# Encoder trunk: the gate and up weight sums, their loads' queue, and how the fourth sum is formed

## The chip, the cores and the metric

The kernel runs on one core of one Trainium2 chip. The metric is device time of one launch in microseconds. The profiler's page and views come from one execution of it.

## The reference, cut to what matters

A two-layer encoder on 528 tokens (16 learned meta tokens and 512 inputs) of width 1024. Each layer is a feed-forward block, a mixer (gated linear attention beside softmax attention), and a second feed-forward block:

```python
def swiglu(x, w_gate, w_up, w_down):
    return (jax.nn.silu(x @ w_gate) * (x @ w_up)) @ w_down

for l in range(DEPTH):
    h = h + 0.5 * swiglu(rmsnorm(h, norm_gains[l, 0]),
                         ffn_w_gate[l, 0], ffn_w_up[l, 0], ffn_w_down[l, 0])
    h = h + mixer(rmsnorm(h, norm_gains[l, 1]), w_in[l], ...)
    h = h + 0.5 * swiglu(rmsnorm(h, norm_gains[l, 2]),
                         ffn_w_gate[l, 1], ffn_w_up[l, 1], ffn_w_down[l, 1])
return rmsnorm(h, final_norm)[:, N_META:]
```

So there are four feed-forward blocks, with D_MODEL 1024 and D_FF 2816, all in float32. The change is in how their weights are prepared.

## The kernel before, in words

**Fast products.** The gate and up products are done by a seven-product scheme for two-by-two blocks in place of eight products. The 2816 hidden channels are 11 pairs of 2 x 128; for each pair a weight matrix is four blocks, 11, 12, 21 and 22, each of 128 x 1024 float32 (512 KB, gate and up together). Products 1, 2 and 4 use the blocks 11, 12 and 22 as they stand (`DIRECT`). The other four use sums: product 7 the third sum s3 = 21 - 11, product 6 the second sum s2 = 22 + s3, product 5 the first sum s1 = 21 + 22, product 3 the fourth sum s4 = s2 - 12. The first two of the three groups of the down product use the same scheme with four sets of sums, numbered 11 to 14. A block of the trunk thus has 15 sets: 11 pairs and 4 down sets; the four blocks have 60.

**The sums are made by DMA.** `negative` (L196 to L199) writes the negated block into a tile of the pool `wsa` (three tiles) on ScalarE. `add` (L201 to L203) is a DMA from GpSimd's queue that adds into its destination (from DRAM or from another SBUF tile). `block` (L188 to L194) loads a block from DRAM on SyncE's queue: direct blocks into the pool `wraw` (three tiles), and the starts of s2 and s1 into the pool `wsb` (two tiles, so the next pair's sums wait for these slots). `sums` strings these together: after product 1's block has been loaded, s3 and s2 and s1; after product 2's weights have been made, s4.

**From float32 to what TensorE takes.** Every block or sum is split in two float32r tiles: ScalarE casts it to `whi` (L252), VectorE subtracts to `wlo` (L253), four tiles of each. A product is then 4 x 2 x 3 = 24 matmuls (L559 for gate and up, L673 for the fast part of down) of 264 columns (256 in the last block).

**Order.** `ffn_steps` writes out the order of the products: pair by pair, interleaved, ..., 6, 5 of a pair, 1 of the next, 7, 2 of the next, 4, 3, then 6 and 5 of the next. `use` makes the weights of up to two products beyond the one in work and fetches nine loads ahead. Each engine's queue runs in order, and which instruction comes first on an engine is decided when the program is built. After products 1, 6 and 7 ScalarE copies the accumulator out of PSUM (L563 and L573), VectorE adds further products to the copy (L569, L579, L586), and then come the gate (L603, L405), the product with up (L613), the split for down (L634, L635), the differences for down (L639) and the additions to the residual `h` (L681).

**What the change touches.** `block` at L193 chooses the queue of the loads; `sums` at L205 to L222 forms the sums; `make` at L257 decides when `sums` is called.

Of the kernel before, what the change touches and what calls it, by code (L numbers as in the profile page):

```python
# [10 lines left out]
F32 = mybir.dt.float32  # L11
# [3 lines left out]
ALU = mybir.AluOpType  # L15
AX = mybir.AxisListType

P = 128
# [14 lines left out]
SLAB = 1024  # L33
# [13 lines left out]
OPENING = ((0, 0), 0), ((0, 0), 1)  # L47
# [96 lines left out]
NPAIR = FF // P // 2  # L144
# [21 lines left out]
class Weights:  # L166
# [21 lines left out]
    def block(self, f, i, name, pool=None, tag="raw"):  # L188

        w = (pool or self.raw).tile([P, SLAB], F32, tag=tag, name=f"w{name}_{f[0]}{f[1]}_{i}")  # L190
        first = f + (i, name) == (0, 0, 0, "11")
        for a in np.split(np.arange(SLAB), 2 if first else 1):
            self.nc.sync.dma_start(w[:, a[0] : a[-1] + 1], self.dram(f, i, name)[:, a[0] : a[-1] + 1])  # L193
        return w  # L194

    def negative(self, f, i, name, w):  # L196
# [8 lines left out]
    def sums(self, f, i, product, w):  # L205


        got = self.summed
        if product == "1":
            s3 = self.negative(f, i, "s3", w)  # L210
            self.add(s3, self.dram(f, i, "21"))
            s2 = self.block(f, i, "22", self.short, "wsb")
            self.add(s2, s3)
            got[f, i, "7"], got[f, i, "6"] = s3, s2
        if (product == "2") == ((f, i) in OPENING):
            s1 = self.block(f, i, "21", self.short, "wsb")
            self.add(s1, self.dram(f, i, "22"))
            got[f, i, "5"] = s1
        if product == "2":
            s4 = self.negative(f, i, "s4", w)  # L220
            self.add(s4, got[f, i, "6"])
            got[f, i, "3"] = s4  # L222

    def fetch(self, upto):
# [13 lines left out]
    def make(self, upto):  # L238
        nc = self.nc
        while self.made < min(upto, len(self.loads)):  # L240
            self.fetch(self.made + 1)
            s = self.made
            load = self.loads[s]
            w = self.raws.pop(s, None)
            if w is None:
                w = self.summed.pop(load)
            hi = self.hi_pool.tile([P, SLAB], F32R, tag="whi", name=f"whi{s}")
            lo = self.lo_pool.tile([P, SLAB], F32R, tag="wlo", name=f"wlo{s}")
            for a in np.split(np.arange(SLAB), 2 if s == 0 else 1):
                cs = slice(a[0], a[-1] + 1)  # L250
                with self.tc.issue_after(self.behind) if self.behind else nullcontext():
                    nc.scalar.copy(hi[:, cs], w[:, cs])  # L252
                nc.vector.tensor_tensor(lo[:, cs], w[:, cs], hi[:, cs].bitcast(F32), ALU.subtract)  # L253
            self.got[s] = (hi, lo)
            self.got.pop(s - 12, None)
            self.made += 1
            if not isinstance(load, int) and (load[2] == "2" or load[2] == "1" and load[:2] in OPENING):  # L257
                self.sums(*load, w)

    def use(self, j, ahead=AHEAD_MADE):  # L260
# [29 lines left out]
def build(tc, ctx, xt, wts, win, par, w2, const, umask, out):  # L290
# [243 lines left out]
    def ffn(l, f, norm, done, following):  # L534

        x, rs, up, n = norm.x, None, None, live[0]
        w = n // 2
        pools = open_pools("left", psum=("s2",), c=4, s2=2)
        made, hid, sums, raw, sets = {}, {}, {}, {}, {}
        risen = iter(range(KC))  # L540

# [636 lines left out]
    def finish_chunk(c):  # L1178
        fin.square(c)
        gain(c, slice(0, SEQ))  # L1180

    def ending(sums, operand, rs):

        table("abs_reciprocal_sqrt_and_small")
# [146 lines left out]
```

## Time and profile before

| | |
|---|---|
| time of three runs | 2295.07, 2302.1, 2309.41 us; median 2302.1 us |
| the profiled execution | 2299.65 us, of which the span is 2297.8 us |
| granted TensorE clock, mean over the span | 0.989 |
| busy over the span | PE 2196.7, VectorE (DVE) 1648.7, ScalarE (ACT) 1289.5, GpSimd (POOL) 210.4 us |
| bytes moved by DMA | 357.56 MB |

PE rows are matmuls, PEld rows weight loads; SPq and POOLq are the queues on which SyncE and GpSimd issue DMAs. A row of the waits tells who waited for whom, the total in us, how often, and the longest. In a timeline a row tells start, duration, engine and line, operation, out<-in, and in brackets how long the engine had been idle before and what ended that. A row of the windows has, for a stretch, the busy time and the number of instructions of PE, PEld, DVE, ACT and POOL, then the granted clock, the busy share of the DMA engines, and GB/s. A row of DMA issues ends with the median us from issue to landing. A row of the groups ends with busy us, mean ns of one, and idle time before. In names of tiles `w` is a block or a sum that began as a load (a direct block, s1 or s2), `s` a sum that began as a negation (s3, s4), `win` the weights in DRAM.

### The profile page before, as it was taken

The page shows a single profiled execution, that of the slowest core. Times are in us where ns is not written, and L with a number is a line of the kernel's source. Part 1 is how long each engine was busy: PE and PEld are TensorE (multiplying, and loading weights), DVE is VectorE, ACT ScalarE, POOL GpSimd, SP SyncE. Part 2 cuts the span into 40 slices and gives each one's busy share as a digit, 9 for nine tenths or more (in the row PEclk, how much of TensorE's full clock was granted, in tenths as well). Part 3 has the DMA queues.
Part 4 walks back from the last instruction along what each step waited for, and adds up shares of the span by engine and source line. Part 5 has one row for each costly group of instructions (what it writes and reads, how often), then busy time and mean ns, then how long its engine had stood idle before and what let it go on. Part 6 is the DMA issues. An engine that isn't in the chain of part 4 may idle for free.

```text
span 2297.8 us, 40260 instructions
## 1 busy us (share of the span) xinstructions
PE 2196.7 (96%) x16506; PEld 2090.2 (91%) x16506; DVE 1648.7 (72%) x2571; ACT 1289.5 (56%) x1867; POOL 210.4 (9%) x244
## 2 busy tenths in 40 slices
PE   7999999999999999989998998999999999999897
PEld 7998999989999998989998988998788888999896
DVE  8875767577976677576687757685779768675857
ACT  8655555345784655555575545553557836555553
POOL 1111110000000011111111111100000001111110
PEclk9999999999999999999999999999999999999999
DMA  9988873212114598888769888832121137888881
GB/s 280 233 208 205 211 184 115 74 47 74 47 38 120 131 223 205 205 206 208 184 155 227 197 204 201 206 106 83 47 73 56 65 111 186 200 220 202 202 218 67
DMA packets 100137, 357.56 MB, mean 156 GB/s; under 512 B 11121, under 2 KB 13553, under 8 KB 99953
## 3 DMA queue, kind: packets, MB, share of 16 engines
q0 software_dynamic: 34560, 125.84, 30.1%
q1 hardware_dynamic: 63440, 226.65, 29.5%
q8 instruction: 130, 2.13, 0.4%
q10 hardware_dynamic: 1952, 2.50, 0.3%
q14 instruction: 55, 0.44, 0.1%
HBM read 289.94 MB, written 2.10 MB: 127 GB/s over the span
## 4 chain that ended last, share of the span: by engine, by line
PE 46%; DMA 26%; DVE 14%; ACT 8%; issue 4%; POOL 0%; SPq 0%; ACTq 0%; POOLq 0%; DVEq 0%
DMA w<-win 14%; PE mm L426 12%; PE ss L426 9%; PE ss L559 9%; DMA s<-w 8%; PE ss L673 7%; DVE wlo L253 4%; DMA s<-win 3%; ACT whi L252 3%; PE sm L426 2%; ACT s L198 1%; PE sm L1034 1%; DVE g L639 1%; DVE h L681 1%; ACT t L405 1%
## 5 line engine op out<-in xcount | busy, mean ns | idle before, releaser
L559 PE MATMUL ss<-xc,whi 128*128 128x264 f32 (+1 forms) x4928 | 918.5, 288 | 40.6 <-ACT c L563 26.6
L559 PEld LDWEIGHTS ss<-xc,whi 128*128 128x128 f32 x4928 | 775.7, 191 | 48.7 <-ACT c L563 30.4
L559 PE MATMUL ss<-xc,wlo 128*128 128x264 f32 (+1 forms) x2464 | 708.4, 288 | 12.5 <-DVE wlo L253 12.4
L253 DVE TENSOR_TENSOR wlo<-w,whi 128x1024 fp32r<-128x1024 f32 (+1 forms) x301 | 365.8, 1218 | 290.6 <-ACT whi L252 289.9
L559 PEld LDWEIGHTS ss<-xc,wlo 128*128 128x128 f32 x2464 | 471.6, 191 | 17.3 <-DVE wlo L253 17.3
L252 ACT CAST whi<-w 128x1024 fp32r<-128x1024 f32 (+1 forms) x301 | 312.4, 1044 | 212.3 <-DMA w<-win 114.8
L426 PE MATMUL mm<-x,whi 128*128 128x264 f32 (+1 forms) x1712 | 384.8, 315 | 0.0
L426 PEld LDWEIGHTS mm<-x,whi 128*128 128x128 f32 x1712 | 278.4, 188 | 16.6 <-issue 1.0
L426 PE MATMUL mm<-x,wlo 128*128 128x264 f32 (+1 forms) x856 | 266.1, 315 | 0.0
L673 PE MATMUL ss<-g,whi 128*128 128x264 f32 (+1 forms) x1280 | 242.3, 287 | 10.3 <-ACT g L634 9.5
L252 ACT CAST whi<-raw 128x1024 fp32r<-128x1024 f32 x126 | 132.1, 1048 | 156.5 <-PE mm L426 102.8
L673 PEld LDWEIGHTS ss<-g,whi 128*128 128x128 f32 x1280 | 200.6, 190 | 15.3 <-ACT g L634 11.1
L253 DVE TENSOR_TENSOR wlo<-raw,whi 128x1024 fp32r<-128x1024 f32 x126 | 153.9, 1221 | 57.6 <-ACT whi L252 56.8
L198 ACT ACTIVATE s<-w 128x1024 f32<-128x1024 f32 x120 | 126.6, 1057 | 109.4 <-DMA w<-win 96.9
L673 PE MATMUL ss<-g,wlo 128*128 128x264 f32 (+1 forms) x640 | 182.3, 285 | 0.0
L426 PE MATMUL ss<-g,whi 128*128 128x264 f32 (+2 forms) x900 | 168.4, 301 | 6.8 <-ACT g L414 5.9
L253 DVE TENSOR_TENSOR wlo<-s,whi 128x1024 fp32r<-128x1024 f32 x120 | 146.5, 1221 | 38.2 <-ACT whi L252 38.2
L426 PEld LDWEIGHTS mm<-x,wlo 128*128 128x128 f32 x856 | 159.6, 188 | 8.5 <-issue 0.7
L426 PEld LDWEIGHTS ss<-g,whi 128*128 128x128 f32 x900 | 132.0, 188 | 14.0 <-ACT g L414 6.9
L563 ACT COPY c<-ss 128x528 f32<-128x528 f32 (+1 forms) x132 | 77.9, 590 | 113.3 <-PE ss L559 112.9
L252 ACT CAST whi<-s 128x1024 fp32r<-128x1024 f32 x120 | 126.0, 1050 | 20.2 <-PE ss L673 19.3
L203 POOL DMA_DIRECT2D w<-win x60 | 54.5, 909 | 901.9 <-DVE wlo L253 384.9
(264 smaller groups left out, 3393.5 us busy)
## 6 DMA issues: line engine op xcount, KB each, us to landing
w<-win SPq DMA_DIRECT2D x299, 512.0 KB, 5.5
raw<-wts SPq DMA_DIRECT2D x126, 512.0 KB, 3.3
s<-win POOLq DMA_DIRECT2D x60, 512.0 KB, 8.0
w<-s POOLq DMA_DIRECT2D x60, 512.0 KB, 5.6
w<-win POOLq DMA_DIRECT2D x60, 512.0 KB, 7.5
s<-w POOLq DMA_DIRECT2D x60, 512.0 KB, 8.7
h<-xt SPq DMA_DIRECT2D x3, 528.0 KB, 6.7
out<-h ACTq DMA_DIRECT2D x4, 256.0 KB, 2.4
```

The costliest lines, as they stand in the source:

```text
L198: self.nc.scalar.activation(t, w, AF.Copy, scale=-1.0)
L203: self.nc.gpsimd.dma_start(t, src, accum_op=ALU.add)
L252: nc.scalar.copy(hi[:, cs], w[:, cs])
L253: nc.vector.tensor_tensor(lo[:, cs], w[:, cs], hi[:, cs].bitcast(F32), ALU.subtract)
L405: prev_act[0] = S.activation(*args, **kw).ins
L426: TE.matmul(acc.half[i][:width], lhs, rhs[:, acc.spans[i]], start=first, stop=last)
L559: TE.matmul(acc[:, j], a[:, j, k], b[:, at], start=bool(begin and k == 0 and i == 0), stop=k == len(x) - 1 and i == 2, skip_group_check=no ...
L563: W.behind = S.copy(part(st, q), acc).ins
L639: V.tensor_tensor(r[into][:, ks], r[a][:, ks], r[b][:, ks], ALU.subtract)
L673: TE.matmul(acc[:, j], a[:, j, k], xs[b][:, k], start=bool(begin and k == 0 and i == 0), stop=k == 3 and i == 2, skip_group_check=not begin)
L681: V.tensor_tensor(to, to, acc, ALU.add)
L1034: TE.transpose(tp[:, j * w + u * n : j * w + (u + 1) * n], pr[:n, (2 * c2 + j) * P : (2 * c2 + j + 1) * P], ident[:n, :n])
```

## The change

All loads into a pool handed to `block` (the starts of s2 and s1, in all 60 sets) are issued from GpSimd's queue; loads of direct blocks stay on SyncE's. For the pairs 2 to 10 of each block (`2 <= i < NPAIR`, 36 of the 60 sets) the block 12 is kept in its raw tile, and when product 6's weights are made, VectorE forms s4 = s2 - 12 in one subtraction; the negation and the accumulating DMA of s4 are gone there. Pairs 0 and 1 and the down sets (11 to 14) form s4 as before.

```diff
--- before.py
+++ after.py
@@ -190,7 +190,7 @@
         w = (pool or self.raw).tile([P, SLAB], F32, tag=tag, name=f"w{name}_{f[0]}{f[1]}_{i}")
         first = f + (i, name) == (0, 0, 0, "11")
         for a in np.split(np.arange(SLAB), 2 if first else 1):
-            self.nc.sync.dma_start(w[:, a[0] : a[-1] + 1], self.dram(f, i, name)[:, a[0] : a[-1] + 1])
+            (self.nc.gpsimd if pool else self.nc.sync).dma_start(w[:, a[0] : a[-1] + 1], self.dram(f, i, name)[:, a[0] : a[-1] + 1])
         return w
 
     def negative(self, f, i, name, w):
@@ -212,13 +212,20 @@
             s2 = self.block(f, i, "22", self.short, "wsb")
             self.add(s2, s3)
             got[f, i, "7"], got[f, i, "6"] = s3, s2
-        if (product == "2") == ((f, i) in OPENING):
+        if product == "12"[(f, i) in OPENING]:
             s1 = self.block(f, i, "21", self.short, "wsb")
             self.add(s1, self.dram(f, i, "22"))
             got[f, i, "5"] = s1
-        if product == "2":
+        late = 2 <= i < NPAIR
+        if product == "2" and not late:
             s4 = self.negative(f, i, "s4", w)
             self.add(s4, got[f, i, "6"])
+            got[f, i, "3"] = s4
+        if product == "2" and late:
+            self.kept = w
+        if product == "6" and late:
+            s4 = self.long.tile([P, SLAB], F32, tag="wsa", name=f"s4_{f[0]}{f[1]}_{i}")
+            self.nc.vector.tensor_tensor(s4, w, self.kept, ALU.subtract)
             got[f, i, "3"] = s4
 
     def fetch(self, upto):
@@ -254,7 +261,7 @@
             self.got[s] = (hi, lo)
             self.got.pop(s - 12, None)
             self.made += 1
-            if not isinstance(load, int) and (load[2] == "2" or load[2] == "1" and load[:2] in OPENING):
+            if not isinstance(load, int) and (load[2] in "26" or load[2] == "1" and load[:2] in OPENING):
                 self.sums(*load, w)
 
     def use(self, j, ahead=AHEAD_MADE):
```

## The prediction

> **What bounds the kernel now.** First the page: its engines' shares, its queues and the chain.
>
> ```profile
> span 2297.8 us, 40260 instructions
> q0 software_dynamic: 34560, 125.84, 30.1%
> q1 hardware_dynamic: 63440, 226.65, 29.5%
> ...
> PE 46%; DMA 26%; DVE 14%; ACT 8%; issue 4%; POOL 0%; SPq 0%; ACTq 0%; POOLq 0%; DVEq 0%
> DMA w<-win 14%; PE mm L426 12%; PE ss L426 9%; PE ss L559 9%; DMA s<-w 8%; PE ss L673 7%; DVE wlo L253 4%; DMA s<-win 3%; ACT whi L252 3%; PE sm L426 2%; ACT s L198 1%; PE sm L1034 1%; DVE g L639 1%; DVE h L681 1%; ACT t L405 1%
> ```
>
> TensorE is nearly always busy, yet a quarter of the chain is DMA, and nearly all of that is the weight sums (w<-win, s<-w, s<-win). The windows tell how much there is to win: the first 30 us, then the product stages of the four feed-forward blocks, then a stretch without a stall.
>
> ```profile
> 0.00:30.00 30.00, 17.85 (x97) 15.25 (x98) 22.55 (x45) 25.62 (x44) 4.76 (x9) 1.00 0.97 287
> 30.00:325.00 295.00, 283.79 (x2257) 279.50 (x2256) 213.11 (x264) 169.81 (x204) 47.54 (x55) 0.99 0.89 221
> 765.00:1110.00 345.00, 328.38 (x2614) 323.35 (x2614) 238.15 (x307) 191.63 (x234) 51.19 (x59) 0.99 0.83 203
> 1150.00:1490.00 340.00, 318.90 (x2528) 313.12 (x2527) 241.12 (x313) 188.55 (x233) 48.19 (x55) 0.99 0.81 199
> 1905.00:2240.00 335.00, 317.44 (x2510) 308.94 (x2509) 231.25 (x298) 185.62 (x226) 50.72 (x58) 0.97 0.85 206
> 900.00:950.00 50.00, 50.00 (x410) 49.79 (x409) 31.86 (x36) 23.85 (x27) 7.85 (x9) 1.00 0.88 213
> ```
>
> In the four stages PE idles 11.2 + 16.6 + 21.1 + 17.6 = 66.5 us, and the clock that is not granted costs 1% of 980 us and 3% of 335 us, 19.9 us: 86 us in all. The undisturbed stretch gives the pace: 50 us / 410 = 0.122 us for a matmul, 24 of them or 2.93 us for a product, seven products or 20.5 us for a pair.
>
> Next, who keeps PE waiting, and who keeps the queue on SP waiting.
>
> ```profile
> PE ss L559 <- ACT c L563: 26.6, 18, 3.5
> PE ss L559 <- DVE wlo L253: 12.4, 21, 0.8
> PE ss L673 <- ACT g L634: 9.5, 7, 1.8
> PE ss L673 <- DVE c L635: 8.4, 14, 0.9
> PE ss L673 <- DVE g L613: 6.1, 6, 2.1
> ...
> SPq L193 <- DVE wlo L253: 593.5, 142, 13.2
> SPq L193 <- DMA s<-w: 334.3, 43, 12.4
> ACT s L198 <- DMA w<-win: 96.9, 30, 5.9
> ```
>
> PE waits for short ScalarE copies (L563) that are done late. SP waits 43 times for `s<-w`, the fourth sum's accumulation, because that DMA reads the second sum's tile, whose slot the next load wants. The timelines of POOL, SP, ACT and PE at the end of the first block's second group show it. By the order of the code the five POOL rows are pair 6's fourth sum, pair 7's second, first and fourth sums, and the next block's third sum.
>
> ```profile
> 197.34 0.86 POOL L203 DMA_DIRECT2D s<-w  x1 [8.37 <-DMA s<-win]
> 204.17 0.89 POOL L203 DMA_DIRECT2D w<-s  x1 [5.96 <-DMA w<-win]
> 212.39 0.88 POOL L203 DMA_DIRECT2D w<-win  x1 [7.33 <-DMA w<-win]
> 212.99 1.17 POOL L203 DMA_DIRECT2D s<-w  x1
> 220.26 0.87 POOL L203 DMA_DIRECT2D s<-win  x1 [6.10 <-DMA s<-w]
> ...
> 206.97 1.85 SPq L193 DMA_DIRECT2D w<-win  x3
> ...
> 194.93 1.05 ACT L252 CAST whi<-w 128x1024 fp32r<-128x1024 f32 x1 [4.89 <-DMA w<-win]
> 195.89 1.05 ACT L198 ACTIVATE s<-w 128x1024 f32<-128x1024 f32 x1
> 217.85 1.05 ACT L252 CAST whi<-w 128x1024 fp32r<-128x1024 f32 x1 [6.35 <-DMA w<-win]
> ...
> 226.67 0.70 PE L559 MATMUL ss<-xc,whi 128*128 128x264 f32 x2 [3.52 <-ACT c L563]
> ...
> 2130.53 0.50 PE L559 MATMUL ss<-xc,whi 128*128 128x256 f32 x2 [1.97 <-ACT c L563]
> ```
>
> This is a ring. The first sum of pair 6 is cast at 194.93; behind it on ACT stands the negation for the fourth sum (195.89); its DMA goes out at 197.34; when it has landed, SP may load the next first sum (206.97); the load lands and the accumulation goes out at 212.39; it lands, and ACT, idle for 6.35 us, casts at 217.85. One turn is 217.85 - 194.93 = 22.9 us, against 20.5 us of matmuls. The 2.4 us add up pair by pair until a lead of two products is spent; then ACT's copy, queued behind that cast, holds PE for 3.52 us.
>
> **The change part by part.** Prices first.
>
> ```profile
> w<-win SPq DMA_DIRECT2D x299, 512.0 KB, 5.5
> raw<-wts SPq DMA_DIRECT2D x126, 512.0 KB, 3.3
> s<-win POOLq DMA_DIRECT2D x60, 512.0 KB, 8.0
> w<-s POOLq DMA_DIRECT2D x60, 512.0 KB, 5.6
> w<-win POOLq DMA_DIRECT2D x60, 512.0 KB, 7.5
> s<-w POOLq DMA_DIRECT2D x60, 512.0 KB, 8.7
> ...
> L198 ACT ACTIVATE s<-w 128x1024 f32<-128x1024 f32 x120 | 126.6, 1057 | 109.4 <-DMA w<-win 96.9
> L253 DVE TENSOR_TENSOR wlo<-s,whi 128x1024 fp32r<-128x1024 f32 x120 | 146.5, 1221 | 38.2 <-ACT whi L252 38.2
> L203 POOL DMA_DIRECT2D w<-win x60 | 54.5, 909 | 901.9 <-DVE wlo L253 384.9
> ```
>
> *Removed.* Of the 15 sets of sums in a block, nine pairs (2 to 10) lose the negation and the fourth accumulation: 36 x 1.06 = 38 us of ACT and 36 DMAs. An accumulation takes 30.1% of 2297.8 us / 240 = 2.88 us of all sixteen DMA engines, a plain transfer 29.5% / about 432 = 1.57 us. A pair's nine transfers took 5 x 1.57 + 4 x 2.88 = 19.4 of 20.5 us; eight take 16.5 us. So transfers should also land sooner. The link from 195.89 to 206.97, 11 us, goes out of the ring.
>
> *Added.* 36 VectorE subtractions of the form of L253, 1.22 us, 44 us; DVE in the four stages goes from some 70% to 74%. Each stands ahead of the next product's `wlo`, so it costs 0 to 1.22 us; I take 0, as weights are made two products (5.9 us) beyond the one in work. If the second sum were late, that lead is gone, and VectorE's additions into `c` and `h` behind it wait too.
>
> *The block held.* The second direct block of a pair stays in its raw slot until the sixth product's weights are made. The block that wants this slot (4 of the same pair) is cast five products later: 14.6 us, less 1.22 for the subtraction and 5.5 for the load, leaves about 8 us. Cost 0; were the lead gone, SP's queue would stand behind that load, and ACT's negation of the next pair's first block with it.
>
> *The loads' queue.* 120 loads move from SP to POOL, which then issues 328 DMAs and set-up rows in place of 244. SP's direct loads no longer stand behind a sum's slot, which should shorten the 96.9 us that ACT's negations wait. On POOL each issue takes 0.9 us, five a pair, 4.5 of 20.5 us. No plain load from POOL is in the trace: it lies between 3.3 us (the quietest load on SP) and 8.0 us (an accumulation from DRAM); I take 5.5, the same transfer's median, for it writes without reading back. The new turn for a first sum is then cast 1.05 + `wlo` 1.22 + load 3.3 to 8.0 + accumulation 7.5 = 13.1 to 17.8 us, 15.3 as taken: below 20.5 even at the dear end. In the order of the changed kernel's POOL instructions a pair reads: third sum, load, load, second sum, first sum (for some pairs the second sum stands between the loads).
>
> The Trainium skill ("SBUF — State Buffer", Who interferes with whom) warns that a load issued from GpSimd can be starved of descriptors while VectorE holds a shared port, and that the SP or ACT queue avoids this. Here a POOL issue took 909 ns with DVE busy 70% of these stages, so the trace shows no starving; by the rule 120 loads could each lose up to one VectorE instruction, and at 1.22 us the turn would be 16.5 us, still below 20.5.
>
> *The start.* Two sum loads of the first pair, formerly in line on SP, now leave POOL at once beside the first blocks. 1.05 MB at the 287 GB/s of the first window is 3.7 us; between 0 and +3.7, I take +2, as the two queues share. *Pairs 0 and 1 and the four down sets* keep their fourth sum; 24 sets with a second issue of 0.9 us in line cost 0 to 22 us; I take +2, since in the rows above issues wait 6 to 8 us for landings, not for POOL.
>
> *The sum.* Of the 86 us I leave 8.4 (L635, fourteen short waits inside the down products) and, of the 26.6 us on L563, the twelve short ones: the six longest (3.52 the first, 1.97 the last) make 18.3, the others 8.3. That leaves 70 us. The 18.3 I take whole; of the other 51, which has the half clock after each stall and shorter waits with several causes, I take half, 26. So 2299.65 (the profiled execution's time) - 44 + 2 + 2 = **2260 us**. Its time stands 2.4 us below the runs' median of 2302.1.
>
> **The rivals.**
>
> *Everything comes back.* All 70 us and no dear start: about 2234. For it: ring and DMA load fall together; against: several stalls have ACT waiting for the next pair's direct block as well.
>
> *A second cause stands behind the first.* The ACT waits of 96.9 us for direct blocks remain, the copies stay late, and nothing is won: 2299.65 + 4 = 2304. For it: 30 such waits of up to 5.9 us; against: SP's queue gets 120 loads shorter, and these loads were what stood before them.
>
> *POOL's one queue becomes the ring (slower).* The loads stand behind the third sum in one queue in order: 8.0 + 2 x 1.6 = 11.2 us for the first sum's load, then its accumulation behind the second's, 7.5 + 2.9 = 10.4, and 2.27 for cast and `wlo`: 23.9 us a turn. It decides from load plus accumulation of 20.6 us on (22.9 - 2.27). The loss grows from 2.4 to 3.4 us a pair, 70 x 3.4 / 2.4 = 99 us, so 2299.65 + 29 + 4 = 2333. For it: a shared queue lets nothing overtake; against: the third sum can leave before the slots are free, as it waits for none of them.
>
> **How the numbers follow.** Forecast 0.62, all back 0.10, second cause 0.14, POOL's ring 0.14. A measurement of this kernel tells about 1%, 23 us, from no change. The first two are faster (0.72), the third the same (0.14), the last slower (0.14). The likeliest case's own range is 2234 to 2280: 18.3 us won and the dear start at one end, everything at the other. The range reaches up over the second cause to 2310 and leaves out most of POOL's ring.
>
> **What would show it.** Right: SP's waits for `s<-w` fall from 43 to the few of pairs 0 and 1 and the down sets; the L563 waits of PE lose those of 2 us and more; PE's idle time in the four stages falls from 66 to about 30 us; L198 counts 84; the subtraction's waits on DVE are short. Wrong: ACT still idles 4 to 6 us a pair for `w<-win`; POOL's loads land after 8 us or more; PE waits for DVE behind the subtraction; the first 30 us hold far fewer than 97 matmuls.

## The result, and the profile after

The changed kernel takes 2273.97 us (median of four runs, 2268.96 to 2280.39) against 2298.6 us for the kernel before, run beside it on the same chip (median of four, 2295.07 to 2309.41). The ratio is 0.9887, 95% interval [0.9843, 0.993]: 1.1% faster, some 25 us, where 2260 was forecast. The profiled execution after is the slowest of its four, 2280.39 us; before it was 2299.65.

The page of after, in the lines that answer to those of before:

```profile
span 2278.6 us, 40100 instructions
q0 software_dynamic: 46656, 169.89, 33.9%
q1 hardware_dynamic: 46160, 163.73, 21.2%
...
PE 60%; DMA 13%; DVE 12%; issue 8%; ACT 6%; POOL 1%; SPq 0%; DVEq 0%; POOLq 0%; ACTq 0%
PE ss L566 24%; PE mm L433 14%; DMA w<-win 10%; PE ss L433 9%; PE ss L680 4%; DVE wlo L260 3%; PE sm L433 2%; DMA w<-s 2%; ACT whi L259 1%; PE sm L1041 1%; DMA s<-w 1%; PE ss L1016 1%; POOL w L203 1%; ACT s L198 1%; PE sm L1057 1%
```

All lines of the code stand 7 lower than before (L559 is now L566, L563 is L570, L673 is L680). DMA's share of the chain has halved, from 26% to 13%, and `s<-w` has almost gone from it, as forecast. But the span is only 19 us shorter. The windows, cut at the same matmuls as those of before (and the first 30 us), tell why:

```profile
0.00:30.00 30.00, 16.43 (x86) 14.04 (x87) 21.95 (x44) 24.84 (x43) 4.38 (x10) 1.00 0.87 268
31.39:337.20 305.81, 287.48 (x2256) 282.75 (x2255) 222.35 (x272) 162.23 (x194) 55.89 (x75) 0.97 0.80 203
776.16:1119.08 342.92, 327.37 (x2614) 323.26 (x2613) 251.31 (x323) 186.61 (x229) 60.67 (x81) 0.99 0.77 195
1154.96:1492.57 337.61, 320.90 (x2528) 315.57 (x2526) 251.46 (x323) 182.83 (x226) 56.05 (x74) 0.98 0.74 187
1906.45:2225.16 318.71, 308.88 (x2509) 303.16 (x2508) 243.44 (x311) 183.17 (x223) 57.80 (x76) 0.99 0.79 202
```

The fourth stage went from 335 to 319 us, but the first is *longer* (305.8 against 295), and PE still idles 18.3 + 15.6 + 16.7 + 9.8 = 60 us in the four, against 66 before. Old stalls went and new ones came. The waits name both:

```profile
PE ss L680 <- DVE h L688: 18.5, 8, 4.3
PE ss L566 <- ACT whi L259: 13.4, 4, 8.9
PE ss L566 <- ACT c L570: 9.9, 11, 1.7
...
SPq L193 <- DVE s L228: 183.4, 28, 14.5
...
DVE s L228 <- DMA w<-s: 39.5, 12, 5.9
```

The long waits for the ScalarE copy are gone (26.6 us and 3.5 at most before, 9.9 and 1.7 now); of the row for `whi`, 8.9 us are the start and 3.5 the opening's stall, below. On top stands a wait that is not among those of before: PE for VectorE's additions into `h`. The subtraction (L228) itself waited twelve times, up to 5.9 us, for the second sum (`w<-s`). SP in turn waited 28 times for the subtraction, which frees the raw tile of block 12.

**The ring is gone.** Two ScalarE rows from the same place as in the prediction; by the order of the code they are the casts of the first sums of pairs 6 and 7:

```profile
205.06 1.05 ACT L259 CAST whi<-w 128x1024 fp32r<-128x1024 f32 x1 [0.31 <-PE ss L566]
...
225.55 1.06 ACT L259 CAST whi<-w 128x1024 fp32r<-128x1024 f32 x1 [0.26 <-PE ss L566]
```

One turn is 20.5 us, the pace of PE itself, and what ends ScalarE's wait is no longer a DMA but PE. Before it was 22.9 us, and the wait was for the sum.

**The new stall.** The handover from the first block's first group to its second, all engines. The rows are pair 4's load of the second sum, its accumulation, PE's last matmul ahead of the gap, the subtraction, the cast, the addition into `h`, and PE's next matmul:

```profile
143.49 1.18 POOL L193 DMA_DIRECT2D w<-win  x2 [0.30 <-issue]
149.99 0.89 POOL L203 DMA_DIRECT2D w<-s  x1 [5.33 <-DMA w<-win]
...
154.22 0.28 PE L680 MATMUL ss<-g,wlo 128*128 128x264 f32 x1
156.80 1.23 DVE L228 TENSOR_TENSOR s<-w,w 128x1024 f32<-128x1024 f32 x1 [5.89 <-DMA w<-s]
156.82 1.05 ACT L259 CAST whi<-w 128x1024 fp32r<-128x1024 f32 x1 [2.97 <-DMA w<-s]
157.94 0.70 DVE L688 TENSOR_TENSOR h<-h,ss 128x528 f32<-128x528 f32 x1
...
158.79 0.78 PE L680 MATMUL ss<-g,whi 128*128 128x264 f32 x2 [4.29 <-DVE h L688]
```

VectorE stands idle for 5.89 us with the subtraction at the head of its queue, because the second sum has not landed. The addition into `h`, whose operands were ready, stands behind it; PE wants the accumulator that this addition empties and waits 4.29 us. Then the clock halves:

```profile
156.90:163.73 6.83, 4.94 (x22) 4.97 (x23) 4.63 (x5) 0.97 (x1) 0.56 (x1) 0.50 1.02 247
163.73:170.00 6.27, 6.27 (x54) 6.27 (x53) 2.00 (x3) 2.49 (x3) 0.86 (x1) 1.00 0.60 157
```

**A ledger.** Both kernels execute 16,506 matmuls, so the start of the k-th can be subtracted from the start of the k-th before; where the difference steps, time was lost or won. In three parts, from the two traces: at the gate and up matmuls among the first 654 (100 us, the opening) +8.7 us; in the down products that end a block's first and second groups (eight of them, the handovers) +30.7; in all the rest, the few other matmuls of the opening included, -58.6. The sum is -19.2 us, the difference of the spans. Outside the opening and the handovers PE's idle time fell from 63.2 to 27.3 us and the time lost to a clock not granted from 20.0 to 4.9 us: 51 of the 58.6.

The opening's loss is 1.5 us until the first matmul and some 7 us at one place:

```profile
29.72 0.86 POOL L203 DMA_DIRECT2D s<-w  x1 [6.35 <-ACT c L570]
...
37.77 1.18 POOL L193 DMA_DIRECT2D w<-win  x2 [6.30 <-DVE t L471]
45.08 0.90 POOL L203 DMA_DIRECT2D w<-s  x1 [6.13 <-DMA w<-win]
49.94 1.04 ACT L259 CAST whi<-w 128x1024 fp32r<-128x1024 f32 x1 [4.85 <-DMA w<-s]
51.04 0.80 PE L566 MATMUL ss<-xc,whi 128*128 128x264 f32 x2 [3.52 <-ACT whi L259]
```

Pair 1's sum loads leave POOL at 37.77. The slot that they take is free when pair 0's fourth accumulation (29.72) has landed, at 37.13 by the record of that transfer; the row of the load names a VectorE instruction that ended at about that time. The chain of load, accumulation and cast then makes PE wait 3.52 us, and half clock follows.

### The profile page after: what moved, and what is told of

The parts are those of the page before. It is cut to its first block, busy times and chain, and to the rows that moved or that the text cites. A ratio compares the mean times of both kernels' runs of the same rounds, so it can differ in the third digit from the quotient of the medians.

```text
span 2278.6 us, 40100 instructions
## 1 busy us (share of the span) xinstructions
PE 2188.9 (96%) x16506; PEld 2088.3 (92%) x16506; DVE 1685.8 (74%) x2607; ACT 1262.7 (55%) x1831; POOL 246.1 (11%) x328
## 4 chain that ended last, share of the span: by engine, by line
PE 60%; DMA 13%; DVE 12%; issue 8%; ACT 6%; POOL 1%; SPq 0%; DVEq 0%; POOLq 0%; ACTq 0%
PE ss L566 24%; PE mm L433 14%; DMA w<-win 10%; PE ss L433 9%; PE ss L680 4%; DVE wlo L260 3%; PE sm L433 2%; DMA w<-s 2%; ACT whi L259 1%; PE sm L1041 1%; DMA s<-w 1%; PE ss L1016 1%; POOL w L203 1%; ACT s L198 1%; PE sm L1057 1%
## 5 line engine op out<-in xcount | busy, mean ns | idle before, releaser
L566 PE MATMUL ss<-xc,whi 128*128 128x264 f32 (+1 forms) x4928 | 905.6, 285 | 25.6 <-ACT whi L259 13.4
L566 PEld LDWEIGHTS ss<-xc,whi 128*128 128x128 f32 x4928 | 767.1, 189 | 30.8 <-ACT whi L259 14.3
L566 PE MATMUL ss<-xc,wlo 128*128 128x264 f32 (+1 forms) x2464 | 702.1, 285 | 3.7 <-DVE wlo L260 3.7
L566 PEld LDWEIGHTS ss<-xc,wlo 128*128 128x128 f32 x2464 | 466.3, 189 | 5.8 <-DVE wlo L260 5.8
L680 PE MATMUL ss<-g,whi 128*128 128x264 f32 (+1 forms) x1280 | 250.9, 294 | 29.2 <-DVE h L688 17.2
L680 PEld LDWEIGHTS ss<-g,whi 128*128 128x128 f32 x1280 | 206.8, 196 | 35.9 <-ACT whi L259 19.5
L570 ACT COPY c<-ss 128x528 f32<-128x528 f32 (+1 forms) x132 | 78.5, 595 | 224.3 <-PE ss L566 224.1
L680 PE MATMUL ss<-g,wlo 128*128 128x264 f32 (+1 forms) x640 | 186.1, 291 | 0.7 <-DVE wlo L260 0.7
L193 POOL DMA_DIRECT2D w<-win x120 | 69.1, 576 | 1079.9 <-DVE x L422 731.2
L259 ACT CAST whi<-s 128x1024 fp32r<-128x1024 f32 x120 | 126.1, 1051 | 22.7 <-PE ss L680 15.3
L433 PEld LDWEIGHTS ss<-g,whi 128*128 128x128 f32 x900 | 131.7, 188 | 5.3
L680 PEld LDWEIGHTS ss<-g,wlo 128*128 128x128 f32 x640 | 125.3, 196 | 1.0 <-DVE wlo L260 1.0
```

What stands on the lines that cost most here:

```text
L193: (self.nc.gpsimd if pool else self.nc.sync).dma_start(w[:, a[0] : a[-1] + 1], self.dram(f, i, name)[:, a[0] : a[-1] + 1])
L433: TE.matmul(acc.half[i][:width], lhs, rhs[:, acc.spans[i]], start=first, stop=last)
L566: TE.matmul(acc[:, j], a[:, j, k], b[:, at], start=bool(begin and k == 0 and i == 0), stop=k == len(x) - 1 and i == 2, skip_group_check=no ...
L570: W.behind = S.copy(part(st, q), acc).ins
L680: TE.matmul(acc[:, j], a[:, j, k], xs[b][:, k], start=bool(begin and k == 0 and i == 0), stop=k == 3 and i == 2, skip_group_check=not begin)
```

## The experiments

Theory A: the ring ran through the slot that the fourth accumulation holds; the subtraction opens it; the losses come from the subtraction at the head of VectorE's queue (handovers) and from the loads in POOL's queue (opening). Theory B: the move of the loads to POOL made the gain. Ledgers below are opening / handovers / rest, in us against before, each from one profiled execution; the times are medians.

**1. Only the subtraction.** Loads back on SyncE's queue:

```diff
-            (self.nc.gpsimd if pool else self.nc.sync).dma_start(w[...], ...)
+            self.nc.sync.dma_start(w[...], ...)
```

> Only the subtraction: all loads of weight sums go back to SyncE's queue. Theory A (the ring ran through the fourth sum's DMA, so its going is the whole gain; the opening was dearer only because of the moved loads): the gains of about 58 us at the ends of the groups stay, the six stalls of some 28 us behind the subtraction stay, the 8.6 us lost before 60 us go, so 2299.65 - 58 + 28 = 2270 us, and the PE stall of 3.52 us near 47.5 us is gone. Theory B (the loads' move did it: on SP they stand behind each other's slots and hold up the direct blocks): most of the 58 us is not there and the time is 2295 or more, with SP's waits in front of the loads long again.

Measured: 2254.03 us against 2300.0, ratio 0.9808 [0.9786, 0.9829]; ledger +0.7 / +9.9 / -57.3. B falls: the gain in the rest is the same without the moved loads. A's 2270 was too high: the handovers lose a third of what they lost. The waits of this kernel and of number 4 (the subtraction behind `wlo`, lines one lower):

```profile
PE ss L680 <- DVE h L688: 11.8, 8, 2.5
```

```profile
PE ss L681 <- DVE h L689: 1.3, 2, 0.7
```

So the stall at a handover needs two things: the subtraction in front, and a late second sum. With the load on POOL the sum lands later still: the subtraction waits up to 5.9 us for it in place of 4.1, and PE up to 4.3 us in place of 2.5.

**2. Only the loads' queue.** All fourth sums by negation and DMA:

```diff
-        late = 2 <= i < NPAIR
+        late = False
```

> Only the loads' queue: the loads of weight sums leave from GpSimd's queue, and every fourth sum is formed by negation and accumulating DMA as before. Theory A (ring through the fourth sum's DMA): the ring is still closed, now through POOL's queue, where more stands in line; the copies are late as before or later, and the opening costs its 8.6 us: 2299.65 + 8.6 = 2308 or more; no PE wait for the additions into h, since there is no subtraction ahead of them. Theory B (the loads' move did it): 2299.65 - 58 + 8.6 = 2250 us.

Measured: 2334.36 us against 2300.0, ratio 1.0146 [1.0126, 1.0166]; +9.0 / +10.9 / +15.0. Slower by 34 us, where A said 8.6 or more. The ring runs on, through POOL's queue now. POOL's rows (pair 6's fourth sum, pair 7's load and accumulation of the first sum), then ScalarE's casts of the two first sums, the first with the negation behind it:

```profile
207.08 0.86 POOL L203 DMA_DIRECT2D s<-w  x1 [6.52 <-ACT s L198]
...
214.39 0.56 POOL L193 DMA_DIRECT2D w<-win  x1 [5.90 <-DMA s<-w]
...
218.97 0.90 POOL L203 DMA_DIRECT2D w<-win  x1 [1.23 <-DMA w<-win]
```

```profile
204.64 1.05 ACT L259 CAST whi<-w 128x1024 fp32r<-128x1024 f32 x1 [2.52 <-DMA w<-win]
205.60 1.05 ACT L198 ACTIVATE s<-w 128x1024 f32<-128x1024 f32 x1
...
228.29 1.05 ACT L259 CAST whi<-w 128x1024 fp32r<-128x1024 f32 x1 [3.74 <-DMA w<-win]
```

A turn is 228.29 - 204.64 = 23.65 us, longer than the 22.9 of before.

**3. The opening's loads on SyncE.** The changed kernel, but pairs 0 and 1 of the first block load their sums from SP:

```diff
-            (self.nc.gpsimd if pool else self.nc.sync).dma_start(...)
+            (self.nc.gpsimd if pool and (f, i) not in OPENING else self.nc.sync).dma_start(...)
```

> The changed kernel, with the four sum loads of the first block's pairs 0 and 1 back on SyncE's queue. Theory A (POOL's in-order queue held pair 1's second load behind pair 0's fourth accumulation): the 8.6 us lost before 60 us come back, first matmul at about 7.4 us, no PE stall near 47.5 us, so 2280.4 - 8.6 = 2272 us in the profiled execution; the rest of the ledger is unchanged. Rival (the opening is slower because the transfers share the DMA engines, whatever the queue): the first matmul comes earlier but the stall near 47.5 us stays, 2277 to 2280 us.

Measured: 2265.36 us against 2300.0, ratio 0.9848 [0.9828, 0.9869]; +1.2 / +25.0 / -59.6. The opening's loss is gone, with PE's stall there, and the first 30 us hold 99 matmuls. The medians stand 8.6 us apart, as expected, but the profiled executions 14.0: the handovers, too, lost 5.7 us less. The cause is not wholly isolated: with the loads' move some of the first instructions of ScalarE, VectorE and TensorE change places too.

**4. The subtraction behind `wlo`.** In the changed kernel it is issued after VectorE's split of the second sum, in all 36 pairs; at the handovers the additions into `h` then stand ahead of it:

```diff
-            self.nc.vector.tensor_tensor(s4, w, self.kept, ALU.subtract)
+            with self.tc.issue_after(self.split):
+                self.nc.vector.tensor_tensor(s4, w, self.kept, ALU.subtract)
...
-                nc.vector.tensor_tensor(lo[:, cs], w[:, cs], ..., ALU.subtract)
+                self.split = nc.vector.tensor_tensor(lo[:, cs], w[:, cs], ..., ALU.subtract).ins
```

> The changed kernel, with the subtraction issued behind VectorE's wlo of the second sum, so that at the handover from the first to the second group the additions into h stand ahead of it. Theory A (the subtraction waits for the late second sum at the head of VectorE's in-order queue, and the additions into h behind it hold PE's accumulators): the PE waits for DVE h of 18.5 us go to under 4 us, the half clock after them too, in all 28 us: 2280.4 - 28 = 2252 us. Rival C (the second sum itself is late, and PE would wait for its weights anyhow): PE's waits move to wlo or whi of the sixth product and the time stays at 2274 to 2282 us.

Measured: 2245.6 us against 2300.0, ratio 0.9771 [0.9748, 0.9794]; +4.3 / -0.7 / -57.6. 28 us below the changed kernel in medians, the gain that A said. The wait for `h` is the row of 1.3 us above, and the subtraction itself no longer waits at all:

```profile
L229 DVE TENSOR_TENSOR s<-w,w 128x1024 f32<-128x1024 f32 x36 | 43.9, 1218 | 0.0
```

**5. The kernel before with a third slot.** No subtraction, no moved queue; one more tile for the first and second sums:

```diff
-        pools = open_pools("left", wsa=3, wsb=2)
+        pools = open_pools("left", wsa=3, wsb=3)
```

> The kernel before, with nothing but a third tile in the pool of the first and second sums (wsb 3 in place of 2). The traffic, the negations and the queues are those of before; only the slot that the fourth sum's accumulation holds is no longer the one that the next load wants. Theory A (a ring through that slot was the limit): most of the 58 us at the ends of the groups comes back, 2299.65 - 58 = 2242 to 2260 us, and SP's waits for s<-w fall from 43 to a few. Rival (the gain comes from the ninth transfer of a pair being gone, 2.88 us of the DMA engines, and from ACT's 38 us): the slot frees nothing that is scarce, 2290 to 2300 us.

Measured: 2247.18 us against 2297.16, ratio 0.9776 [0.9742, 0.9809]; +0.7 / -12.6 / -35.5. The time is A's. PE, VectorE and ScalarE execute the same instructions in the same order as before; only the sums' loads stand earlier on SP, and some neighbours on POOL change places. The ring was the slot, not the ninth transfer nor ScalarE's 38 us: with both of those still there, more is won than by the change. The same two casts as above, now 19.5 us apart, the second waiting for PE and no DMA:

```profile
195.31 1.05 ACT L252 CAST whi<-w 128x1024 fp32r<-128x1024 f32 x1 [1.30 <-DMA w<-win]
...
214.82 1.06 ACT L252 CAST whi<-w 128x1024 fp32r<-128x1024 f32 x1 [0.31 <-PE ss L559]
```

One expectation failed. Waits of SP and of ScalarE:

```profile
SPq L193 <- DMA s<-w: 284.2, 42, 12.5
```

```profile
ACT whi L252 <- DMA w<-win: 24.0, 11, 4.8
```

SP still waits 42 times for `s<-w`. With three tiles a load takes the slot of three loads ago in place of two, so it waits for an older sum, and a queue that fetches ahead waits for some slot in any case. The count of such waits is no sign of a ring. The sign is the consumer's wait, which fell to this 24.0 us; in the kernel before, the same row reads

```profile
ACT whi L252 <- DMA w<-win: 114.8, 27, 7.6
```

**6 and 7. The subtraction behind `wlo`, with all loads on SyncE (6), and with the opening's loads alone there (7).** The edits are those of numbers 1 and 4, and of 3 and 4.

> The subtraction alone (all loads on SyncE's queue), issued behind VectorE's wlo of the second sum. The subtraction alone still lost 9.9 us against before in the down products at the ends of the first and second groups, in the three blocks where it lost. Theory A (what is lost there is the blocked h additions): these come to about nothing, 2254 - 10 = 2244 us. Rival (what is left there is the second sum that lands late): 2250 to 2254 us.

> The changed kernel with both mendings: the subtraction behind wlo, and the opening pairs' loads back on SyncE's queue; the other sets' loads stay on GpSimd's. The two losses are apart in place, so they should add: 2245.6 less the 4.3 us that the kernel with the subtraction behind wlo still loses before 95 us, about 2242 us. If instead the loads on GpSimd's queue still cost something in the stages, this one stays above the subtraction alone behind wlo.

Measured: 2243.15 us against 2297.16, ratio 0.9759 [0.9728, 0.9791], +0.2 / -4.6 / -53.8; and 2244.68 us, ratio 0.9769 [0.9738, 0.98], 0.0 / +2.8 / -60.3. Both as expected. The two and number 4 cannot be told apart by their intervals, so once the subtraction blocks nobody, the loads' queue is worth nothing that shows.

**8. The subtraction twice.** Number 4, with the subtraction issued a second time into the same tile.

> The changed kernel with the subtraction behind wlo and done twice: 36 more VectorE instructions of 1.22 us into the same tile, 44 us of VectorE, nothing else. Theory A (VectorE's added work lies under the lead of two products and costs nothing when it blocks nobody): 2245.6 us within 5 us. Rival (each subtraction pushes the wlo behind it and what PE waits for): 10 to 44 us more, 2256 to 2290 us, with PE's waits for DVE c, wlo and h longer.

Measured: 2258.86 us against 2297.16, ratio 0.983 [0.9796, 0.9864], 13 us above number 4. The time is not A's and lies at the low end of the rival's range, but the rival's sign is missing: PE's waits for `h` are 1.3 us as in number 4, those for `c` and `wlo` 7.2 and 4.0 us against 7.4 and 5.2. So it is not a clean price. The order of ScalarE's and PE's instructions changed with the edit, and what PE waits for is again the copy (10.4 us in number 4):

```profile
PE ss L568 <- ACT c L572: 32.2, 11, 4.5
```

What VectorE's second 44 us cost apart from that order stays open.

**9 to 11. The third slot on top:** of number 6 (9), of the changed kernel (10), and of number 2 (11). The edit is that of number 5.

> The subtraction alone, behind wlo, loads on SyncE's queue, and the third tile for the first and second sums besides. If the slot and the subtraction open the same ring, they do not add: 2235 to 2247 us, at most some 8 us below either alone (2243.2 and 2247.2), from sums that start earlier. If fewer transfers and less ScalarE work have a worth of their own once the ring is open, the two add more: 2225 us or less.

> The changed kernel with a third tile for the first and second sums. The loads no longer wait for a slot, so the second sum is made earlier, and the subtraction finds it landed at the handovers: the 28 us of blocked h additions go, the opening's 8.6 us may stay: 2245 to 2255 us. If the second sum is late at the handovers because of what stands ahead of its load in GpSimd's queue, and not because of the slot, the stalls stay: 2268 to 2275 us.

> The loads on GpSimd's queue, fourth sums by negation and DMA, and a third tile for the first and second sums. If the loads alone cost 34 us because the ring through the slot runs on through GpSimd's queue, the third slot takes that and the old ring away: about the 2247.2 us of the kernel before with a third slot, plus 8.6 us at the opening, 2250 to 2260 us. If GpSimd's queue is dear in itself (everything behind an accumulation that waits), most of the 34 us stays: 2270 to 2285 us.

Measured against 2300.22: 2247.18 us, ratio 0.9768 [0.9747, 0.979]; 2250.15 us, ratio 0.9776 [0.9755, 0.9797]; 2276.76 us, ratio 0.9897 [0.9875, 0.9918]. The slot and the subtraction do not add (number 9 stands at the upper edge of what was expected): they open the same ring. On the changed kernel the slot also takes the handovers' loss from +30.7 to -3.5, with the subtraction still in front: PE's waits for `h` fall to 1.3 us, as the second sum starts early enough. The loads on POOL with negation and DMA stay 30 us above number 5 (2247.18): there the queue is dear in itself. Some 11 us of it are lost at the opening (+12.1 against +0.7); the rest goes with ScalarE's wait for the sums, 24.0 us in number 5 and here

```profile
ACT whi L259 <- DMA w<-win: 100.6, 25, 8.8
```

The loads' move by itself, in medians:

| how the fourth sum is made | loads on SP | loads on POOL | the move costs |
|---|---|---|---|
| negation and DMA, two slots | 2297 to 2300 | 2334.4 | +34 |
| negation and DMA, three slots | 2247.2 | 2276.8 | +30 |
| subtraction in front | 2254.0 | 2274.0 | +20 |
| subtraction behind `wlo` | 2243.2 | 2245.6 | +2 |

No median went below 2243 us; 4, 5, 6, 7 and 9 lie within some 4 us of each other, all about 2.3% under the kernel before and 27 to 31 us under the changed one. The cheapest of them is number 5, which is one digit.

## Why the prediction was right, and where its steps were not

The sign and the range held, and the diagnosis is shown: the ring through the fourth sum's slot was what bounded the four stages (numbers 1 and 5 open it in two ways, and number 9 shows that the two do not add). The median lay 14 us above the forecast. In the profiled execution the sum was 2299.65 - 44 + 2 + 2; the ledger has -58.6 + 30.7 + 8.7. Three terms were mis-sized, and the gain taken too small covers some 15 of the 35 us of losses that were missed. That the median came within 14 us is in part luck.

*The gain, 44 taken, 58 measured.* The six long copy waits went, as said. To take half of the other 51 was too careful: the half clock after the stalls and the short waits went with them, as the ledger's idle time and clock show.

*The subtraction, 0 taken, about 28 measured.* This is the step that failed. "I take 0, as weights are made two products (5.9 us) beyond the one in work" holds inside a group. At a handover the second sum lands late, and the sentence that followed, "If the second sum were late, that lead is gone, and VectorE's additions into `c` and `h` behind it wait too", is word for word what the trace shows, for `h`. It stood there as a warning, got no price and was no rival. Number 4 shows the price in this kernel; with the loads on SP the same subtraction in front costs 11 us (number 1 against 6), so the moved loads are part of it. What was missed was to look at each group's end, where loads, handover and down product crowd together, for how early the second sum lands; the turn inside a group does not tell it.

*The start, +2 taken, 8.7 measured.* The shared queue at time 0 costs 1.5 us, within its bounds of 0 to 3.7. The other 7 us come from pair 1's loads behind pair 0's accumulations; I had priced the opening's first transfers, not the second pair.

*The block held, 0 taken.* This step holds: SP waits for the subtraction in number 4 as well (32 times, 199.7 us in all, against 28 and 183.4), and that kernel is among the fastest.

*The loads' queue.* The turn of a first sum was put at 15.3 us, and with the subtraction the casts keep PE's pace, so that step holds. But the move was taken for a relief of SP: ScalarE's waits for direct blocks did fall from 96.9 to 55.1 us in after, yet with the loads on SP (number 1) they are 72.3 us and the kernel is 20 us faster, and in number 5 they are 148.4 us and it is 27 us faster. The relief was of something that bound nothing. The +2 us for a second issue in line were not measured apart.

*The slower rival*, POOL's queue as the ring, was priced at 23.9 us a turn and 2333 us. It did not occur in the changed kernel. Number 2 has a ring of 23.65 us and 2334.4 us; the numbers meet, but the path is another: its load waits for the fourth sum's landing, which the changed kernel no longer has. *The second cause* is refuted, since the copies came in time. *Everything comes back* did not occur in this kernel, for the new stalls.

Two slips of the working change nothing here. The upper end of the likeliest case, 2280, does not come out of its terms: 2299.65 - 18.3 + 3.7 + 2 is 2287. And the last of the five POOL rows (220.26) is by the order of the code the third sum of a down set.

*The signs.* Right: ScalarE's copies no longer hold PE for 2 us or more, and L198 counts 84. The loads' issue is cheap too:

```profile
L198 ACT ACTIVATE s<-w 128x1024 f32<-128x1024 f32 x84 | 88.6, 1057 | 66.9 <-DMA w<-win 55.1 <-DVE wlo L260 11.5
L193 POOL DMA_DIRECT2D w<-win x120 | 69.1, 576 | 1079.9 <-DVE x L422 731.2 <-DVE wlo L260 167.0 <-issue 65.7
```

Wrong: PE's idle time in the four stages fell to 60 us and not to about 30, the subtraction's waits were not short and PE waited for VectorE behind it, and the first 30 us hold 86 matmuls in place of 97. These signs were on the list, and they pointed at the two dear terms. SP's waits for `s<-w` did vanish, but this sign proves nothing: the loads that had them left SP, and in number 5 they stay while the ring is open.

The Trainium skill ("SBUF — State Buffer", Who interferes with whom) spoke against loads from GpSimd for fear of starved descriptors. The same section of the Trainium skill holds, as an inference, that `tensor_tensor`, VectorE's operation in the subtraction and in `wlo`, does not block the writing of descriptors. The trace agrees: the row above, 576 ns an issue with DVE at 74% of the span, shows no starving, and number 4 against number 6 shows no cost. The Trainium skill's advice to use SP's queue was the better choice here by 20 us all the same, but for another reason: the order within one queue.

## What to carry to other kernels

Before replacing an operation to break a ring through a buffer, try one more buffer: it tells whether the ring is the bound, and here it won more than the rewrite. An instruction added to an in-order engine can cost far more by what stands behind it while its operand is late than by its length: here 28 us in front of ready work, and nothing that shows behind it, though a second 44 us of it was not free (number 8). Price it at the latest arrival of that operand, at the ends of groups, not at the steady pace, and put it behind work that is already ready. Moving transfers to another queue moves what they stand behind: ask for each which wait is now ahead of it.

## What the runs showed of the hardware

A plain load from GpSimd's queue costs 0.58 us to issue, less than the 0.9 us of an accumulation, and it lands not much later than one from SP: the medians in after are

```profile
w<-win POOLq DMA_DIRECT2D x180, 512.0 KB, 6.1
w<-win SPq DMA_DIRECT2D x179, 512.0 KB, 5.4
```

where the first row has 60 accumulations among its 180.

The clock halves after short stalls too. The handover at 290 us idled PE for 2.21 us, and soon after it 3.4 us ran at half clock:

```profile
292.31 0.49 PE L680 MATMUL ss<-g,whi 128*128 128x264 f32 x2 [2.21 <-DVE h L688]
```

```profile
293.43:296.85 3.42, 3.42 (x18) 3.42 (x18) 1.62 (x2) 0.00 (x0) 0.56 (x1) 0.50 1.05 216
```

In the trace of after each of the eight stalls of 2.0 to 4.3 us after the first matmul has such a stretch of 3.4 or 6.8 us with it, and none of the five of 1.5 to 1.74 us has one. It is no sharp bound: in number 3 a stall of 2.33 us has none, and in before one of 1.75 us has.
